# Order of the logits and of the preceding chunk's values inside one TensorE operation of a local attention

## The chip, the cores and the metric

The kernel runs on one core of one Trainium2 chip. The metric is the device time of one execution in microseconds, as the median of several runs. The engines are TensorE (PE in the profile, its weight loads PEld), VectorE (DVE), ScalarE (ACT), GpSimd (POOL) and SyncE (SP), which issues nearly all DMAs.

## The reference, cut to what matters

One decoder layer on x of 2048 tokens by 1024 channels, all in float32. Behind an RMS norm, one projection makes the columns of two head groups that run side by side: a retention (4 heads) and a sliding-window softmax attention (8 query heads, 2 key heads, head size 64, window 128). Each group is gated, the groups are concatenated, projected back and added to x. The change lies in the second group:

```
logits = einsum('bnqhgd,bnkhd->bhgnqk', qb, kband) * 64**-0.5
logits = where(mask, logits + bias, -1e30)          # 0 <= distance < 128
probs  = softmax(concatenate([logits, sink], -1))[..., :-1]
out    = einsum('bhgnqk,bnkhd->bnqhgd', probs, vband)
```

The 2048 tokens are cut into 16 chunks of 128, and a chunk's queries see their own chunk and the one before.

## The kernel before, in words

Four projections (512, 384, 512 and 512 columns wide) take most of the time. Each is made by Strassen's scheme from seven block products for each of 8 pairs of chunks; each of those is 12 matmuls of 128x128 tiles (the float32 operands are split into a high and a low part by ScalarE and VectorE, and three of the four combinations are multiplied). Their results land in PSUM tiles named `acc`; operand tiles are named `x` and `w`. 56 such block products make one projection, and a "turn" in the constants below is one of them.

Between these products TensorE does the small work: transposes, retention (`update`, `retain`) and the local attention (`window`, `attend`, `values`, `outputs`). Small matmuls use parts of the array as separate tiles: the logits (`m<-ks,qT` in the profile) contract 64 rows into 32 columns, the values (`m<-side,vb` and `m<-last,vb`) contract 32 rows into 64 columns, retention uses 64 by 64.

For chunk c, `attend` does this: q is multiplied by its norm's factors on VectorE (`qn`), turned by DMA (`apart`, a store to `planes_dram`, a transposing DMA into `qT`); the keys are turned by TensorE (`m<-ident,kn`) and written by ScalarE into `ks_t`; then one TensorE operation, labelled "logits", is planned for both the values of chunk c - 1 and the logits of chunk c. It takes four PSUM banks `pls`. The logits are 64 matmuls that fill columns 0 to 319 of the banks, banks 0 and 1 in their first half and banks 2 and 3 in their second. The values are 80 matmuls that fill columns 320 to 447: five blocks, one after the other, each over all four banks. Behind it VectorE adds the bias and takes the row's extreme from each bank (`lg<-m,bias,nsnk`, 8 instructions), ScalarE takes the exponential, VectorE turns the blocks (`side`, `last`), and ScalarE copies the four banks' values out (`so`). Chunk 0 has logits alone, and the values of chunk 15 are an operation of their own.

The order of the instructions on every engine is written out ahead, by a planner in the kernel's own code (`Program.emit`). Each operation has a cost for each engine that may do it (how long it occupies the engine, how long until its result is there), a due time in turns, and buffers from pools with shares (`SHARE`). The planner walks through a modelled time and takes the operation that can go first; TensorE's products follow in their fixed order, and small operations are put between them. Where a group of small matmuls follows another such group, it may start `INSIDE` us after its inputs are there; behind a product it is `SETTLED` us. `WIN`, `RET` and `GATE` give the due times of the local attention, of the retention and of the gates, with a base, a step for each chunk or pair, and small amounts by which single ones are moved (`WIN_BY`, `RET_BY`, `GATE_BY`). `EARLIER_Q` moves q's load and its turning ahead of the chunk's due time, `EARLIER_U` does that for retention's state update. `small()` is the planned cost of a small VectorE operation, `VALUES` that of the values.

Every instruction is issued through one helper, so that the profile has line 434 for all of them; groups are told apart by the names of their tiles.

Of the kernel before, what the change touches and what calls it, by code (L numbers as in the profile page):

```python
# [56 lines left out]
CAP = {"k": 93, "h": 8, "bank": 8}  # L57
SMALL, COUNTS = 3, {"ms": 1, "rxt": 1, "rqk0t": 1, "rqk1t": 1}

SHARE = {"x": 14, "raw": 38, "acc": 21, "wr": 20, "wh": 20, "att": 36, "ret": 19, "rin": 14, "gate": 10, "mix": 37, "norm": 7, "res": 6, "turned": 7, "first": 5, "block": 4, "rest": 6}  # L60

HELD = 6
FIRST_X, SPLIT_X = 2.5, 0.4
SHARE["held"] = 2 * HELD

# [34 lines left out]


LATER, CROWD, MOST, SOONER = 15.0, 2.5, 4, 35.0
SETTLED, INSIDE = 0.5, 0.25


def change(a, b):
# [55 lines left out]
class Program:  # L162
# [5 lines left out]
    def op(self, cost, go, r=(), w=(), due=0.0, table=None, label="", also=()):  # L168

        o = Op()  # L170
        o.cost, o.go, o.due, o.after, o.set, o.label = cost, go, due, [], table, label
        o.n, o.left, o.ready, o.end, o.seen, o.by, o.count = len(self.ops), 0, 0.0, 0.0, 0.0, None, 0
        deps = set()
        for b in r:
            if b.writer is not None:
                deps.add(b.writer)
        for b in w:
            if b.writer is not None:
                deps.add(b.writer)
            deps.update(b.readers)  # L180
        for b in r:
            b.readers.append(o)
        for b in w:
            b.writer, b.readers = o, []
        o.bufs = list(dict.fromkeys((*r, *w, *also)))
        for b in o.bufs:
            b.left += 1
        o.new = [b for b in (*w, *also) if b.ap is None and b.tag]
        for d in deps:
            if d is not o:  # L190
                d.after.append(o)
                o.left += 1
        self.ops.append(o)
        return o

    def emit(self):
# [5 lines left out]
        slots = {t: [(0.0, i) for i in range(n)] for t, n in cap.items()}  # L202
        used = dict.fromkeys(SHARE, 0)
        count = len(self.ops)
# [10 lines left out]
        while done < count:  # L215
            best = None
            for e, found in avail.items():
# [4 lines left out]
                for due, n, o in found[:48]:  # L222
# [28 lines left out]
                    for tag, bs in need.items():  # L251
# [7 lines left out]
                        for share in {b.share for b in bs if b.share}:  # L259
                            many = used[share] + sum(b.share == share for b in bs)  # L260
                            if many > SHARE[share] - (spare if share in SPARED else 0):
                                short = True
# [94 lines left out]


TURNED = {"q": range(NCH), "qk": range(NCH), "weights": (), "gated": (2, 4, 6, 7, 10, 12, 14)}
EARLIER_Q, EARLIER_K, EARLIER_U, LATER_W = 0, 1.5, 2.5, -1.0  # L360


def dve(n, two=False, lat=0.08):
# [13 lines left out]


def small(n=1):
    return {"V": (0.14 * n, 0.22 * n, True)}  # L380


def f32r(n, count):
# [4 lines left out]
def f32(n, count):  # L388
    t = count * (n / 600 + 0.01)
    return {"T": (t, t + 0.25, False)}  # L390
# [12 lines left out]
BANDS_DUE, VALUES = 0.0, 1.45  # L403
# [36 lines left out]
def layer(ctx, tc, xt, xfirst, xtok, nw, w_in, w_rn, qkw, sinks, biasg, rope, decays, dmask, gpow, w_out, out):  # L440
    nc = tc.nc
    order = Order(tc)
    V, G, A, Q, T = (Engine(order, e) for e in (nc.vector, nc.gpsimd, nc.scalar, nc.sync, nc.tensor))
# [19 lines left out]
    def kb(name, share, dtype=F32):  # L463
        return Buf("k", None, dtype, name, share)
# [7 lines left out]
    def ps(share="rest", name="m"):  # L472
        return Buf("bank", None, F32, name, share)

    def fixed(shape, name, dtype=F32):
        return Buf(name=name, ap=const.tile(shape, dtype, name=name))
# [11 lines left out]
    def load(b, src, due, kbytes=256, to=lambda t: t, cost=None, also=(), of=lambda t: t):  # L488
        op(
            cost or dma(kbytes), lambda e: e.dma_start(to(b()), of(src())), [src], [b], due, label=f"load {b.name}",  # L490
            also=also,
        )
# [32 lines left out]
    wr = fixed([P, 4], "wr")  # L525
# [359 lines left out]
    def spill(to, n):  # L885
        def sink(p, row, col, b, due):
            store(to[col][2 * p + row], b, due + 4, n // 2, lambda t: t[:, :n])
        return sink
# [347 lines left out]
    def values(c, chunk, vs, banks):  # L1236

        sides, lasts, o, parts = chunk  # L1240

        def go(e):
            by = "p (i q) -> p i q"
            for j in range(5):
                for u, r in enumerate(QUARTERS):
                    for g, to in enumerate((L, H)):
                        v, at = (vs[c], j * P) if j < 4 else (vs[c + 1], 0)
                        if j < 4:
                            w = sides[g]()[r, :].rearrange("p (i k) -> p i k", k=P)[:, :, j * 32 : j * 32 + 32]
                        else:  # L1250
                            w = lasts()[r, o + g * P : o + (g + 1) * P].rearrange(by, q=32)
                        e.matmul(
                            banks[u]()[to, 320 : 320 + P].rearrange(by, q=32), v()[r, at + g * 64 : at + g * 64 + 64], w,
                            start=j == 0, stop=j == 4, skip_group_check=True,
                        )

        return go, [*parts, vs[c], vs[c + 1]], (*sides, lasts)
# [82 lines left out]
    def attend(c, a, b, fac, facs, due, bias_t, ks_t, nsnk, held, vs):  # L1340
# [5 lines left out]
        def go(e):  # L1346
            e.tensor_tensor(
                qn().rearrange(hd, d=HD), a().rearrange(hd, d=HD), fac()[:, 0:8].unsqueeze(2).to_broadcast([P, 8, HD]),
                ALU.mult,
            )  # L1350

        soon = due - (EARLIER_Q if c in TURNED["q"] else 0)
        op(both(512), go, [a, facs], [qn], soon, label="qn")

        def go(e):
            for g in range(KVH):
                e.activation(
                    kn()[:, g * HD : (g + 1) * HD], b()[:, g * HD : (g + 1) * HD], AF.Copy, scale=fac()[:, 8 + g : 9 + g]
                )

        op({"A": (0.47, 0.57, False)}, go, [b, facs], [kn], due, label="kn")

        pk, pq = ps(), ps()
# [6 lines left out]
        if c in TURNED["q"]:  # L1370
            turn_by_dma(qn, qT, planes_dram[2][c], soon + 0.1)
        else:

            def go(e):
                for i in range(4):
                    e.transpose(pq()[:, i * P : (i + 1) * P], qn()[:, i * P : (i + 1) * P], ident())

            op(turns(4), go, [qn, ident], [pq], due + 0.2, "small", label="turn q")
            op({"A": act(512)}, lambda e: e.activation(qT(), pq(), AF.Copy), [pq], [qT], due + 0.35, label="qT")
# [18 lines left out]
        parts = []  # L1398

        pls = [ps() for _ in range(4)]  # L1400
        before, reads, also = values(c - 1, held[-1], vs, pls) if held else (None, [], ())

        def go(e):
            if before:
                before(e)
            for t in range(2):
                for j in range(2):
                    for u, q in enumerate(QUARTERS):
                        for g, r in enumerate((L, H)):
                            o = (2 * t + j) * P + u * 32  # L1410
                            e.matmul(
                                pls[2 * t + g]()[q, j * 160 : j * 160 + 160], qT()[r, o : o + 32],
                                ks_t()[r, slot * 256 + u * 32 : slot * 256 + u * 32 + 160], start=True, stop=True,
                                skip_group_check=True,
                            )

        t = f32(160, 4)["T"][0] + (VALUES - 0.23 if before else 0)
        op(
            {"T": (t, t + 0.25, False)}, go, [qT, ks_t, *reads], [*pls, passed], due + 0.5, "eighths", label="logits", also=also,
        )  # L1420
        for bank, heads in enumerate([(2 * t + j, g) for j in range(2)] for t in range(2) for g in range(2)):
            later, n = due + 0.5 + 0.2 * bank, len(heads)
# [20 lines left out]
            def go(e, lg=lg, heads=heads):  # L1443
# [9 lines left out]
                also=(nm, den),  # L1453
            )
            t, g = bank // 2, bank % 2
            most = Part(sides[g], lambda s, t=t: s[:, t * 256 : t * 256 + 256])
            rest = Part(lasts, lambda s, t=t, g=g: s[:, o + g * P + t * 64 : o + g * P + t * 64 + 64])
# [63 lines left out]
    def gates(p, row, col, b, due):  # L1521

        c = 2 * p + row
        if row == col == 0:
            store(g_dram[p], b, due)
            g = kb("g", "gate")
            due = GATE[0] + p * GATE[1] + GATE_BY[p]
            load(g, g_dram[p], due - 4)
            gate(0, c, due, g)
        else:  # L1530

            need = 3 * n7 + (THREES.at[1 + col, p] if row else THREES.first[6] - 4 + 1.4 * p)
            gate(col, c, max(due + 0.5, GATE[0] + 0.5, need - LEAD), b)

# [45 lines left out]
    products(B1, W1, 384, n7, TWOS, spill(rq_dram, 384))  # L1580
    window(lambda c: WIN[0] + c * WIN[1] + WIN_BY[c])
    retention(lambda c: RET[0] + c // 2 * 2 * RET[1] + c % 2 * 1.0 + RET_BY[c // 2])
    W3 = weights(w_in, 1792, 512, (nw_sb, KT), 2 * n7, TWOS)
# [9 lines left out]


WIN = (47.0, 5.3)
RET = (109.0, 2.85)
GATE = (140.0, 3.8)

WIN_BY = (-1.0, 0.5, -1.5, 0.0, 1.5, 0.5, 1.0, 1.0, -0.5, 1.0, 1.0, 2.0, 0.5, 0.5, 0.0, 2.0)
RET_BY = (-1.5, 0.0, -1.5, 1.0, -1.0, -2.5, -0.5, -1.0)  # L1600
GATE_BY = (-1.5, -0.5, -2.5, -0.5, -0.5, -0.5, 0.0, 0.5)

LEAD = 7.0

# [98 lines left out]
```

## Time and profile before

| | us |
|---|---|
| median of 3 runs | 668.02 (667.99 to 668.63) |
| the profiled execution's own time | 667.38 |
| its span, first to last instruction | 665.6 |
| TensorE busy | 661.2 |
| VectorE busy | 588.2 |
| ScalarE busy | 477.4 |

The page divides the span into 40 slices of 16.6 us. The local attention runs from about 169 to 456 us, the retention from about 314 to 493 us. A row of the timeline gives the start in us from the span's beginning, the time covered in us, the engine, the operation with its tiles and shapes, and a count; brackets hold the engine's idle time just before and what ended it.

### The profile page before, as it was taken

To read this page: it belongs to the slowest core of one execution; us is meant where nothing else is said; L and a number is where in the kernel's file an instruction comes from. 1 tells how busy PE (TensorE), PEld (TensorE's weight loads), DVE (VectorE), ACT (ScalarE), POOL (GpSimd) and SP (SyncE) were. 2 spreads that over 40 slices of the span, in tenths; PEclk is the share of its full clock that TensorE was granted. 3 is DMA by queue.
4 is the path that set the end of the run, shared out by engine and by line. 5 is a ranking of instruction groups with operands and counts; after the bars stand their busy time and mean duration, and the time that the engine had idled before them with its cause. 6 is when DMAs were issued, how large, how long until landed. Compare 5 with 4: busy or idle time off the path is not lost.

```text
span 665.6 us, 16699 instructions
## 1 busy us (share of the span) xinstructions
PE 661.2 (99%) x6072; PEld 561.0 (84%) x6072; DVE 588.2 (88%) x1423; ACT 477.4 (72%) x1177; POOL 15.6 (2%) x39
## 2 busy tenths in 40 slices
PE   9999999999999999999999999999999999999998
PEld 7888888889999999998887888888888888888886
DVE  6999967797788987899999999988899999997862
ACT  7766975577798675698979998999999863353200
POOL 0000000032200000000000000000000000000000
PEclk9999999999999999999999999999999999999999
DMA  9999973789998789999999999898999995126622
GB/s 323 369 327 374 393 258 147 239 305 336 255 312 255 191 257 292 331 302 281 313 286 316 354 268 278 269 261 269 287 308 318 306 282 154 48 95 222 206 95 96
DMA packets 162114, 175.99 MB, mean 264 GB/s; under 512 B 69488, under 2 KB 96240, under 8 KB 162032
## 3 DMA queue, kind: packets, MB, share of 16 engines
q1 hardware_dynamic: 161888, 174.92, 86.7%
q8 instruction: 48, 0.79, 0.5%
q14 instruction: 34, 0.28, 0.1%
q10 hardware_dynamic: 144, 0.00, 0.0%
HBM read 104.03 MB, written 56.43 MB: 241 GB/s over the span
## 4 chain that ended last, share of the span: by engine, by line
PE 99%; DVE 0%; issue 0%
PE acc L434 87%; PE m L434 12%; DVE t L434 0%; DVE none L434 0%
## 5 line engine op out<-in xcount | busy, mean ns | idle before, releaser
L434 PE MATMUL acc<-w,x 128*128 128x512 f32 (+1 forms) x2700 | 588.0, 377 | 0.0
L434 PEld LDWEIGHTS acc<-w,x 128*128 128x128 f32 x2700 | 491.8, 188 | 84.2 <-issue 5.1
L434 DVE TENSOR_TENSOR x<-x 128x512 fp32r<-128x512 f32 (+2 forms) x214 | 140.5, 681 | 9.9 <-ACT x L434 9.5
L434 ACT ACTIVATE x<-x 128x512 fp32r<-128x512 f32 (+1 forms) x181 | 107.2, 616 | 15.2 <-DVE x L434 10.7
L434 DVE TENSOR_TENSOR w<-w 128x512 fp32r<-128x512 f32 (+3 forms) x96 | 61.6, 668 | 0.1
L434 ACT ACTIVATE lg<-lg,nm 128x160 f32<-128x160 f32 x128 | 53.2, 419 | 7.2 <-DVE nm L434 7.1
L434 ACT ACTIVATE w<-w 128x512 fp32r<-128x512 f32 (+1 forms) x72 | 40.9, 602 | 20.8 <-PE acc L434 14.8
L434 DVE TENSOR_TENSOR s<-acc,s 128x512 f32<-128x512 f32 (+1 forms) x64 | 41.8, 654 | 10.0 <-PE acc L434 9.8
L434 DVE SCALAR_TENSOR_TENSOR w<-w,nw_sb 128x512 fp32r<-128x512 f32 (+3 forms) x72 | 49.7, 713 | 0.9 <-ACT w L434 0.9
L434 DVE CUSTOM_DVE_ANT_0 lg<-m,bias,nsnk 128x160 f32<-128x160 f32 x128 | 40.9, 381 | 3.8 <-PE m L434 3.8
L434 DVE TENSOR_TENSOR t<-acc,t 128x512 f32<-128x512 f32 (+2 forms) x33 | 21.0, 636 | 15.9 <-PE acc L434 15.8
L434 ACT ACTIVATE x<-go 128x512 fp32r<-128x512 f32 x40 | 24.2, 630 | 14.8 <-DVE w L434 6.4
L434 ACT ACTIVATE w<-w,nw_sb 128x512 fp32r<-128x512 f32 (+3 forms) x45 | 29.0, 680 | 2.3 <-DMA w<-in_w_in 2.3
L434 DVE STREAM_TRANSPOSE side<-lg 128x256 f32<-128x256 f32 x64 | 28.0, 438 | 2.6 <-ACT lg L434 2.4
L434 DVE TENSOR_TENSOR x<-go,x 128x512 fp32r<-128x512 f32 x40 | 27.5, 694 | 1.1 <-ACT x L434 1.1
L434 ACT ACTIVATE apart<-qn 128x1024 uint16<-128x1024 uint16 x16 | 16.7, 1052 | 14.7 <-DVE qn L434 14.7
L434 DVE TENSOR_TENSOR t<-acc,s 128x512 f32<-128x512 f32 (+1 forms) x32 | 21.3, 665 | 5.1 <-PE acc L434 5.0
L434 ACT ACTIVATE ro<-ro,nmu,rg 128x128 f32<-128x128 f32 x64 | 25.1, 496 | 0.0
L434 DVE TENSOR_TENSOR r<-acc,t 128x512 f32<-128x512 f32 (+1 forms) x32 | 20.9, 653 | 4.4 <-PE acc L434 4.3
L434 ACT ACTIVATION_READ_ACCUMULATOR lg<-lg,nm 128x1 f32 x128 | 24.5, 191 | 0.0
L434 ACT ACTIVATE s<-acc 128x512 f32<-128x512 f32 (+1 forms) x32 | 18.0, 570 | 9.0 <-PE acc L434 8.7
L434 ACT ACTIVATE xk<-xk 128x512 f32<-128x512 f32 x32 | 19.8, 620 | 5.5 <-DMA xk<-in_xtok 5.5
(124 smaller groups left out, 595.1 us busy)
## 6 DMA issues: line engine op xcount, KB each, us to landing
x<-in_xt SPq DMA_DIRECT2D x74, 256.0 KB, 5.2
x<-s_dram SPq DMA_DIRECT2D x64, 256.0 KB, 5.0
planes_dram<-apart SPq DMA_DIRECT2D x55, 256.0 KB, 4.4
w<-in_w_in SPq DMA_DIRECT2D x40, 256.0 KB, 5.4
s_dram<-x SPq DMA_DIRECT2D x32, 256.0 KB, 4.8
xk<-in_xtok SPq DMA_DIRECT2D x32, 256.0 KB, 4.9
res<-in_xtok SPq DMA_DIRECT2D x32, 256.0 KB, 3.8
w<-in_w_out SPq DMA_DIRECT2D x20, 256.0 KB, 4.9
```

The source lines that it names most:

```text
L434: return self.order.put(op(*a, **k))
```

## The change

Inside the common TensorE operation of a chunk, the matmuls of the logits are issued first and those of the preceding chunk's values behind them; both still go to the same four PSUM banks, and the operation still needs all its inputs before it is planned. With it, constants of the planner are changed: two shares of buffers, `INSIDE`, `EARLIER_Q`, `EARLIER_U`, the cost of small VectorE operations, the cost of the common operation, and the due times of retention, of the gates and of one chunk of the window.

```diff
-SHARE = {"x": 14, "raw": 38, "acc": 21, ...
+SHARE = {"x": 15, "raw": 35, "acc": 21, ...
...
-SETTLED, INSIDE = 0.5, 0.25
+SETTLED, INSIDE = 0.5, 0.1
...
-EARLIER_Q, EARLIER_K, EARLIER_U, LATER_W = 0, 1.5, 2.5, -1.0
+EARLIER_Q, EARLIER_K, EARLIER_U, LATER_W = 2.0, 1.5, 1.5, -1.0
...
 def small(n=1):
-    return {"V": (0.14 * n, 0.22 * n, True)}
+    return {"V": (0.17 * n, 0.25 * n, True)}
...
-        before, reads, also = values(c - 1, held[-1], vs, pls) if held else (None, [], ())
+        behind, reads, also = values(c - 1, held[-1], vs, pls) if held else (None, [], ())
 
         def go(e):
-            if before:
-                before(e)
             for t in range(2):
                 for j in range(2):
                     for u, q in enumerate(QUARTERS):
                         for g, r in enumerate((L, H)):
...
+            if behind:
+                behind(e)
+
+        t = f32(160, 4)["T"][0] + (VALUES - 0.31 if behind else 0)
-        t = f32(160, 4)["T"][0] + (VALUES - 0.23 if before else 0)
...
-RET = (109.0, 2.85)
-GATE = (140.0, 3.8)
+RET = (107.0, 2.85)
+GATE = (140.0, 4.0)
...
-WIN_BY = (-1.0, 0.5, -1.5, 0.0, 1.5, 0.5, 1.0, 1.0, -0.5, 1.0, 1.0, 2.0, 0.5, 0.5, 0.0, 2.0)
+WIN_BY = (-1.0, 0.5, -1.5, 0.0, 1.5, 0.5, 1.0, 1.0, -0.5, 1.0, 1.0, 2.0, 0.5, -0.5, 0.0, 2.0)
-GATE_BY = (-1.5, -0.5, -2.5, -0.5, -0.5, -0.5, 0.0, 0.5)
+GATE_BY = (-1.5, 0.5, -1.0, 1.0, 1.0, 1.0, 1.5, 2.0)
```

More of the change, by code (lines that the diff above doesn't have):

```diff
@@ L58 @@
 SMALL, COUNTS = 3, {"ms": 1, "rxt": 1, "rqk0t": 1, "rqk1t": 1}
-SHARE = {"x": 14, "raw": 38, "acc": 21, "wr": 20, "wh": 20, "att": 36, "ret": 19, "rin": 14, "gate": 10, "mix": 37, "norm": 7, "res": 6, "turned": 7, "first": 5, "block": 4, "rest": 6}
+SHARE = {"x": 15, "raw": 35, "acc": 21, "wr": 20, "wh": 20, "att": 36, "ret": 19, "rin": 14, "gate": 10, "mix": 37, "norm": 7, "res": 6, "turned": 7, "first": 5, "block": 4, "rest": 6}
 HELD = 6
```

## The prediction

> **What bounds the kernel now.** I read the page first, then TensorE's waits, then the chain of waits, then the timeline around the changed operation. The page:
>
> ```profile
> span 665.6 us, 16699 instructions
> PE 661.2 (99%) x6072; PEld 561.0 (84%) x6072; DVE 588.2 (88%) x1423; ACT 477.4 (72%) x1177; POOL 15.6 (2%) x39
> PEclk9999999999999999999999999999999999999999
> PE 99%; DVE 0%; issue 0%
> PE acc L434 87%; PE m L434 12%; DVE t L434 0%; DVE none L434 0%
> ```
>
> TensorE is busy for 99% of the span at the full granted clock, and the chain that ends last is TensorE almost alone. A busy TensorE can hide waits, so the list of its waits comes next. It has one entry:
>
> ```profile
> PE m L434 <- DVE none L434: 1.2, 1, 1.2
> ```
>
> That one is the warm-up at the start. After it no matmul waits for data, for a bank or for another engine. So the time is the sum of what TensorE issues, plus the few us at the two ends, and an edit can gain only by taking cycles out of TensorE's own stream; it can lose without limit by making TensorE wait. "Earlier" and "later" on other engines are worth nothing until they reach TensorE.
>
> **The changed operation.** The timeline of TensorE around one instance (the common operation of chunk 2), then the first chunk's logits alone, the last chunk's values alone, and a place where other small matmuls stand in front:
>
> ```profile
> 190.99 1.19 PE L434 MATMUL m<-side,vb 32*64 32x128 f32 x63
> ...
> 192.35 1.34 PE L434 MATMUL m<-ks,qT 64*32 64x160 f32 x64
> 193.62 0.80 PE L434 MATMUL acc<-w,x 128*128 128x384 f32 x3
> ...
> 169.28 1.34 PE L434 MATMUL m<-ks,qT 64*32 64x160 f32 x64
> 170.55 0.80 PE L434 MATMUL acc<-w,x 128*128 128x384 f32 x3
> ...
> 454.69 1.19 PE L434 MATMUL m<-side,vb 32*64 32x128 f32 x63
> ...
> 456.06 0.73 PE L434 MATMUL acc<-w,x 128*128 128x512 f32 x2
> ...
> 313.80 1.10 PE L434 MATMUL m<-v,qk 64*64 64x128 f32 x32
> 314.84 1.19 PE L434 MATMUL m<-side,vb 32*64 32x128 f32 x63
> ...
> 316.20 1.34 PE L434 MATMUL m<-ks,qT 64*32 64x160 f32 x64
> ```
>
> The first column is the start; I count each part from its first start to the next part's, so that it carries the gap behind it. Values: 192.35 - 190.99 = 1.36 us with the logits behind, 456.06 - 454.69 = 1.37 with a product behind, 316.20 - 314.84 = 1.36 with retention's matmuls in front. Logits: 193.62 - 192.35 = 1.27 with the values in front, 170.55 - 169.28 = 1.27 with a product in front. Each part costs the same whoever its neighbours are.
>
> **The swap on TensorE.** It moves 80 value matmuls behind 64 logit matmuls in 15 operations; it adds none and removes none, and moves no DMA by itself. Before: 1.36 + 1.27 = 2.63. After: 1.27 + 1.36 = 2.63, if a part's closing gap depends on that part alone. One seam never occurs in the trace: logits followed by values, from tiles of 64x32 to tiles of 32x64. Its bounds come from retention's matmuls, with a switch of tile size behind them and without:
>
> ```profile
> 398.73 1.10 PE L434 MATMUL m<-v,sT 64*64 64x128 f32 x32
> 399.76 0.74 PE L434 MATMUL acc<-w,x 128*128 128x512 f32 x2
> ...
> 329.55 1.10 PE L434 MATMUL m<-v,sT 64*64 64x128 f32 x32
> 330.48 1.05 PE L434 MATMUL m<-v,qk 64*64 64x128 f32 x32
> 331.46 0.72 PE L434 MATMUL acc<-w,x 128*128 128x512 f32 x2
> ```
>
> With a switch the 32 matmuls take 1.03 us, without one 0.93: a switch costs 0.10. If the new seam had none, each operation would save 0.10, and 15 x 0.10 = 1.5 us; if it cost a second one, it would lose as much. The nearest rows are the two seams into or out of the value matmuls (64x64 to 32x64: 314.84 - 313.80 = 1.04; 32x64 to 64x32: the same 1.36 as to a product). Both pay the switch in full. I take 0.00, and keep -1.5 and +1.5 as ends.
>
> **Stalls inside the operation.** The chain of waits lists the operation in 2.63 us nearly everywhere, and longer in three places:
>
> ```profile
> 250.74 2.63 PE m L434 x142
> 266.18 2.96 PE m L434 x142
> ...
> 287.13 2.76 PE m L434 x141
> ...
> 381.58 2.71 PE m L434 x139
> ```
>
> The excess is 0.33 + 0.13 + 0.08 = 0.54 us. The weight loads show the first as a pause in the middle of the logits, with nothing waited for:
>
> ```profile
> 267.47 0.70 PEld L434 LDWEIGHTS m<-ks,qT 64*32 64x32 f32 x42 [0.17 <-issue]
> 268.40 0.42 PEld L434 LDWEIGHTS m<-ks,qT 64*32 64x32 f32 x22 [0.23 <-issue]
> ```
>
> [...] Ends: all gone (-0.5) or twice as many (+0.5). I take 0.0, the nearest being the same number elsewhere.
>
> **VectorE.** The bias instruction reads the logits' bank. In the old order a bank has its last matmul when its logits are through, and two of the four banks are through halfway:
>
> ```profile
> 208.66 0.38 DVE L434 CUSTOM_DVE_ANT_0 lg<-m,bias,nsnk 128x160 f32<-128x160 f32 x1 [0.93 <-PE m L434]
> ...
> 209.06 0.80 PE L434 MATMUL acc<-w,x 128*128 128x384 f32 x3
> ...
> DVE lg L434 <- PE m L434: 3.8, 4, 1.4
> ```
>
> The first bias of chunk 3 starts at 208.66, 0.40 before the operation's end at 209.06. In the new order the values fill columns 320 to 447 of each bank last of all (the loop over the five value blocks is outside, that over the banks inside), so if the program guards a whole bank, the first bias comes at the operation's end, about 0.45 later than now; if it guards the columns, it comes 1.36 sooner. [...] No row here tells the two apart, and I take the later one. VectorE waits for these logits in 4 chunks only (last row), one of which is chunk 0, without values; the others are 3, 5 and 6. Chunk 2's bias starts before the operation's end as well:
>
> ```profile
> 193.24 0.38 DVE L434 CUSTOM_DVE_ANT_0 lg<-m,bias,nsnk 128x160 f32<-128x160 f32 x1
> ```
>
> (193.24 against 193.62.) Elsewhere the bias comes after the operation and doesn't feel the swap, so 4 x 0.45 = 1.8 us of new waiting on VectorE. Queued behind it are the splits of x and w, which feed the products. What hides it is VectorE's spare time there:
>
> ```profile
> core 0: us, PE busy (x) PEld busy (x) DVE busy (x) ACT busy (x) POOL busy (x), PEclk, DMA share, GB/s
> 175.00:260.00 85.00, 85.00 (x1260) 80.73 (x1259) 73.78 (x234) 65.76 (x212) 0.00 (x0) 1.00 0.91 262
> ...
> 310.00:420.00 110.00, 110.00 (x1612) 88.76 (x1611) 108.03 (x338) 101.76 (x277) 0.00 (x0) 1.00 1.07 298
> ```
>
> In the stage of those chunks it is idle for 85.00 - 73.78 = 11.2 us, so I take 0.0, with +1.8 as the end without cover. From 310 to 420 us it has only 2.0 us to spare, but there the queue ahead of the bias is longer than the operation.
>
> **The planner's constants.** They move no arithmetic, only the order. x gets one more buffer and raw tiles three fewer; q (its loads, the products with its factors, its turning DMAs) goes two turns earlier, retention's base two, its state update one turn later, and the gates up to 2 + 0.2 x 7 = 3.4 turns later; small VectorE operations are planned 0.03 longer; the common operation is planned 0.08 shorter and, next to another small-matmul operation, may follow its inputs by 0.10 instead of 0.25. On SP the 16 q loads (256 KB, 4.7 us to land), 16 stores and 16 turning DMAs come in front of some loads of x:
>
> ```profile
> x<-s_dram SPq DMA_DIRECT2D x64, 256.0 KB, 5.0
> ...
> aq<-aq_dram SPq DMA_DIRECT2D x16, 256.0 KB, 4.7
> ```
>
> TensorE feels any of this in two ways. Neighbouring groups of small matmuls may fuse or come apart: a fusion saves at least the 0.10 of a switch and at most both idle times of the weight loader around a group (0.35 going in, 0.17 coming out, together 0.52):
>
> ```profile
> 398.73 0.86 PEld L434 LDWEIGHTS m<-v,sT 64*64 64x64 f32 x32 [0.35 <-issue]
> 399.76 0.53 PEld L434 LDWEIGHTS acc<-w,x 128*128 128x128 f32 x3 [0.17 <-issue]
> ```
>
> I take 0.2 (an estimate; part of the idle time lies under the product still running). Retention's earlier base brings one more of its steps under the window operations, so I count one fusion more: -0.2. Or a load comes late and TensorE waits: 0.0 here, since it has no wait now; the end is one missed landing of 5.0 us.
>
> **Sum.** 0.0 (seam) + 0.0 (pauses) + 0.0 (VectorE) - 0.2 (order) = -0.2 us against the profiled execution's own 667.4 us (span 665.6 and 1.8 around it): 667.2. The median of the runs is 668.02, 0.6 above that execution, so the forecast on that scale is 667.8 us. A change under 0.2% (1.3 us) can't be told from none by a measurement of this kernel; this is one.
>
> **Rivals.**
> - The seam is free: 1.5 us less, 668.0 - 1.5 - 0.2 = 666.3. For it: the planner now books the operation 0.08 shorter. Against it: all switches in the trace pay. [...] Chance 0.08.
> - The new order is itself the gain: the 0.54 of pauses gone and four more fusions at 0.2, 668.0 - 0.5 - 0.8 = 666.7, at the edge of what is told from none, more if fusions are worth up to 0.52. For it: most retention groups stand apart from the window's. Against it: it needs all of it at once. Chance 0.11.
> - Slower: the bias waits for the whole operation, VectorE stands still for 4 x 0.45 = 1.8 us, and the splits behind reach TensorE late: 668.0 + 1.8 = 669.8. It decides once an operand's split is finished less than 0.45 us before its product. Against it: 11.2 us idle in that stage. Chance 0.11.
> - Slower by SP: one load of x behind the earlier q traffic misses its product by up to a landing: 668.0 + 5.0 = 673.0; the DMA share of 1.07 from 310 to 420 speaks for it, TensorE's empty list of waits against it. Chance 0.07.
> - That the change doesn't do what it says (logits first, readers no earlier) is what I expect, and costs nothing.
>
> **How the numbers follow.** My case, 667.2 to 668.9, has 0.63. The range of 8 in 10 runs from the free seam's 666.3 to the stalled VectorE's 669.8. Faster by over 0.2%: 0.08 + 0.11 = 0.19. Slower: 0.11 + 0.07 = 0.18. Within: 0.63.
>
> **What would show it.** Right: TensorE's list of waits still holds only the warm-up, the logits' first start to the values' is 1.27 and the values' to the next product's 1.36, and the bias of chunk 3 starts at the operation's end or later. The seam fails if the logits take about 1.17 before the values. The VectorE step fails if a bias starts while the value matmuls run. The whole is wrong if TensorE shows a wait for x or w, or if the groups of small matmuls number clearly fewer than now.

## The result, and the profile after

The changed kernel takes 672.03 us (median of 4 runs, 671.45 to 675.22); the kernel before, timed beside it, 668.01 (667.99 to 668.63). The ratio is 1.0071, with a 95% interval of 1.0046 to 1.0097: slower by 4.0 us. I had forecast 667.8 with a range of 666.3 to 669.8, so the forecast and the range were both wrong.

The page of the changed kernel: span, busy times, the chain that ended last by engine, and the group of the bias with the idle time ahead of it.

```profile
span 670.7 us, 16720 instructions
PE 663.1 (99%) x6072; PEld 562.1 (84%) x6072; DVE 587.9 (88%) x1423; ACT 478.4 (71%) x1177; POOL 15.6 (2%) x39
...
PE 84%; ACT 6%; DMA 4%; DVE 3%; issue 2%; SPq 0%; ACTq 0%; DVEq 0%
...
L434 DVE CUSTOM_DVE_ANT_0 lg<-m,bias,nsnk 128x160 f32<-128x160 f32 x128 | 40.8, 380 | 6.1 <-PE m L434 6.1
```

The share of busy time still reads 99%, and no engine has more work: the matmuls are as many (TensorE's busy time is 1.9 us longer for them), VectorE's and ScalarE's busy times are the same within 1 us. What differs is the chain: before, it was TensorE for 99%; now it runs through ScalarE, DMAs and VectorE for 13%, so TensorE waited somewhere. TensorE's list of waits, which held the warm-up alone, names where (us in total, times, longest):

```profile
PE m L434 <- issue: 1.5, 2, 1.0
PE m L434 <- DVE none L434: 1.2, 1, 1.2
PE m L434 <- ACT so L434: 1.1, 1, 1.1
PE acc L434 <- DVE r L434: 0.3, 1, 0.3
```

1.5 + 1.1 + 0.3 = 2.9 us are new. The largest place is one group near 307 us. TensorE's timeline there, then ScalarE's, then VectorE's:

```profile
307.39 1.32 PE L434 MATMUL m<-ks,qT 64*32 64x160 f32 x64
...
310.00 0.43 PE L434 MATMUL m<-v,qk 64*64 64x128 f32 x2
311.41 1.10 PE L434 MATMUL m<-v,qk 64*64 64x128 f32 x30 [0.98 <-issue]
313.62 0.33 PE L434 MATMUL m<-ident,kn 128*128 128x128 f32 x1 [1.12 <-ACT so L434]
313.71 2.54 PE L434 MATMUL acc<-w,x 128*128 128x512 f32 x10
...
310.85 0.41 ACT L434 ACTIVATE lg<-lg,nm 128x160 f32<-128x160 f32 x1
...
313.32 0.74 ACT L434 ACTIVATE so<-m 128x128 f32<-128x128 f32 x4
...
314.46 0.38 DVE L434 COPY state<-m 128x256 f32<-128x256 f32 x1
...
316.48 0.40 DVE L434 TENSOR_TENSOR state<-state,m 128x256 f32<-128x256 f32 x1
317.14 0.41 DVE L434 TENSOR_TENSOR state<-state,m 128x256 f32<-128x256 f32 x1
```

The common operation starts at 307.39. Directly behind it stands retention's first state update (`m<-v,qk`, 32 matmuls), and directly behind that the transpose of the next chunk's keys (`m<-ident,kn`). The update stops after 2 matmuls and goes on at 311.41; the transpose waits until ScalarE begins the four copies `so`, which stand behind six exponentials of 0.41 us. (VectorE takes the update's results out of their two banks later still: from 314.46 on, and as the code reads each bank twice, with the last reads at 316.48 and 317.14.) From the operation's start to the next product it is 313.71 - 307.39 = 6.32 us. Without waits it would be 2.61 + 1.03 + 0.09 = 3.73 (operation, update with its switch, transpose), so 2.6 us are lost.

Before, the same kinds of work met too, in the order update, operation, three matmuls of a product, transpose. The update and the operation (313.80, 314.84 and 316.20) are shown with the prediction; what follows them is

```profile
317.47 0.97 PE L434 MATMUL acc<-w,x 128*128 128x512 f32 x3
318.28 0.27 PE L434 MATMUL m<-ident,kn 128*128 128x128 f32 x1
...
317.17 0.42 DVE L434 TENSOR_TENSOR state<-state,m 128x256 f32<-128x256 f32 x1
```

and nothing waits. There the update stands in front, and the transpose has 318.28 - 314.84 = 3.44 us from the operation's start. By then one of the update's two banks has been read for the last time (the row of VectorE, done at 317.59), so a bank is free without ScalarE's copies; that the transpose takes this bank fits, but no view names the bank.

The weight loader shows smaller waits that the matmuls' list leaves out or counts only in part, these two and one of 0.53 us for ScalarE's `x` at 481:

```profile
357.90 0.97 PEld L434 LDWEIGHTS m<-v,sT 64*64 64x64 f32 x32 [0.40 <-DVE sT L434]
...
394.47 0.86 PEld L434 LDWEIGHTS m<-state,qkT 64*64 64x64 f32 x30 [0.39 <-ACT so L434]
```

The start differs as well. Here are the first products, before and then after:

```profile
4.64 2.53 PE L434 MATMUL acc<-w,x 128*128 128x512 f32 x10
```

```profile
4.79 2.47 PE L434 MATMUL acc<-w,x 128*128 128x512 f32 x5
```

Five matmuls where there were ten, 0.15 us later: about 1.2 us in all. I don't put that down to the change: the same slow start (6 matmuls) is in the profiled execution of a kernel that ran within 0.6 us of the kernel before (the one with the small operations' cost, below), and it is absent (10 matmuls) from the changed kernel with the copies sooner.

The account of the profiled spans, 670.7 - 665.6 = 5.1 us: start +1.2; the group at 307 +2.6; a pause of 0.9 in the operation at 267 against three pauses of 0.54 in all before +0.4; the place at 394 +0.6 and the one at 480 +0.5; waits for masked scores `sT` at 358, 378 and 488 +0.3; the swap itself -0.4 (see the seam, in the section on the prediction). That makes 5.2. The groups of small matmuls, counted in TensorE's timeline, are 33 in both executions, so no fusion enters. The medians differ by 4.0; the account without the start gives as much.

### The profile page after: what moved, and what is told of

Its sections match the earlier page's. It is cut to its first block, busy times and chain, and to the rows that moved or that the text cites. A ratio compares the mean times of both kernels' runs of the same rounds, so it can differ in the third digit from the quotient of the medians.

```text
span 670.7 us, 16720 instructions
## 1 busy us (share of the span) xinstructions
PE 663.1 (99%) x6072; PEld 562.1 (84%) x6072; DVE 587.9 (88%) x1423; ACT 478.4 (71%) x1177; POOL 15.6 (2%) x39
## 4 chain that ended last, share of the span: by engine, by line
PE 84%; ACT 6%; DMA 4%; DVE 3%; issue 2%; SPq 0%; ACTq 0%; DVEq 0%
PE acc L434 76%; PE m L434 8%; DMA planes_dram<-apart 2%; ACT ro L434 1%; ACT lg L434 1%; ACT qk L434 1%; ACT apart L434 1%; DVE w L434 1%; DMA so_dram<-so 1%; DMA w<-in_w_in 1%; ACT x L434 1%; DMA a<-rq_dram 1%; DMA v<-rq_dram 0%; DVE lg L434 0%; ACT w L434 0%
```

## The experiments

Each kernel was timed beside the kernel before; ratios are to that one, with 95% intervals. The first question was whether the order inside the operation costs anything, or the plan around it.

**The swap alone.** The kernel before, with nothing changed but the order of the two parts; all constants, and so the order on every engine, are those of before.

```diff
         def go(e):
-            if before:
-                before(e)
             for t in range(2):
...
+            if before:
+                before(e)
```

> The kernel before with the swap of the matmuls alone: logits first, values behind, every constant of the planner and so every engine's order as before. Theory A (the new plan of the order is what costs): TensorE's operation takes 2.70 us instead of 2.73 by the trace of after, 15 x 0.025 = 0.4 us less, the bias of chunk 3 starts about 0.5 us later, and the whole stays within 1 us of 668.0. Theory B (the swap costs, since the bias and then the copies of the values are held until the operation's end and the banks come free later): 670 to 672 us, with waits of TensorE for ScalarE's copies.

Measured: 667.92 us, ratio 0.9997 (0.9983 to 1.0011). TensorE's one wait besides the warm-up's, and the first bias of chunk 3:

```profile
PE m L434 <- issue: 0.4, 1, 0.4
...
209.27 0.38 DVE L434 CUSTOM_DVE_ANT_0 lg<-m,bias,nsnk 128x160 f32<-128x160 f32 x1 [1.17 <-PE m L434]
```

The bias starts at 209.27 instead of 208.66, 0.6 later, and VectorE waits longer, but TensorE doesn't feel it. In the profiled execution most operations take 2.61 us instead of 2.63, 0.4 us less in all, and two take 3.25 and 3.09 because of pauses. The swap costs nothing and gains nothing that can be told.

**The plan alone.** The changed kernel with the values first again: all constants as changed, the order of the engines as changed.

```diff
         def go(e):
+            if behind:
+                behind(e)
             for t in range(2):
...
-            if behind:
-                behind(e)
```

> The changed kernel with its own plan, but the values first again inside the operation. Theory A (the plan costs): 671 to 672 us, with the pause near 269 us, the pause near 310 us and the waits for the copies near 313 and 394 us still there. Theory B (the swap costs): 668 to 669 us, the waits for the copies gone, because the bias starts 0.4 us or more before the operation's end again.

Measured: 672.82 us, ratio 1.0072 (1.0051 to 1.0093), as for the whole change. TensorE's timeline:

```profile
307.63 1.19 PE L434 MATMUL m<-side,vb 32*64 32x128 f32 x63
...
310.27 1.22 PE L434 MATMUL m<-v,qk 64*64 64x128 f32 x32
313.87 0.39 PE L434 MATMUL m<-ident,kn 128*128 128x128 f32 x1 [2.38 <-ACT so L434]
313.96 4.34 PE L434 MATMUL acc<-w,x 128*128 128x512 f32 x11
```

Again 313.96 - 307.63 = 6.33 us for the group, now without a pause in the update: the transpose waits 2.38 in one piece. So the loss belongs to the changed constants, and the update's pause in the changed kernel only takes time out of a wait that is there anyway. Behind the wait, 11 matmuls take 4.34 us, where 10 took 2.54 in the changed kernel; more on that in the last section.

**Where the pause comes from.** Four matmuls of 256 columns at the start (the warm-up, `WARM` in the code), whose result nothing reads, are replaced by sixteen of 64 columns; the stream of instructions behind them is 48 longer and otherwise the same.

```diff
-        for _ in range(WARM):
-            e.matmul(pw()[:, 0:256], none()[:, 0:P], none()[:, 0:256], start=True, stop=True)
+        for i in range(4 * WARM):
+            e.matmul(pw()[:, 0:64], none()[:, 0:P], none()[:, 0:64], start=True, stop=True)
```

> The changed kernel with the 4 warm-up matmuls of 256 columns replaced by 16 of 64 columns; the order of everything behind is the same, but TensorE's instruction stream is 48 instructions longer ahead of the first product. If the pauses with nothing waited for (0.9 us in the values near 269 us and 1.4 us in retention's matmuls near 310 us) are fetches of instructions, they move or vanish: the next block is asked for 24 matmuls earlier in the stream, 4 us in the products, so both should be gone, 2.3 us, if no other place gets one: 669 to 670 us. If they are waits for data or banks, they stand at the same matmuls with the same lengths, and the time stays 671 to 672 us.

Measured: 676.83 us, ratio 1.0135 (1.0118 to 1.0152). The warm-up itself got dearer: the first product starts at 8.03 us instead of 4.79, and more of the first ones are slow (11 matmuls from 9 to 13 us, where the changed kernel has 19), so the whole time, which I had expected at 669 to 670 us, says nothing about the rest. The places do:

```profile
273.58 1.19 PE L434 MATMUL m<-side,vb 32*64 32x128 f32 x63
...
274.95 0.80 PE L434 MATMUL acc<-w,x 128*128 128x384 f32 x3
...
311.66 1.32 PE L434 MATMUL m<-ks,qT 64*32 64x160 f32 x64
...
314.27 1.10 PE L434 MATMUL m<-v,qk 64*64 64x128 f32 x32
317.96 0.33 PE L434 MATMUL m<-ident,kn 128*128 128x128 f32 x1 [2.59 <-ACT so L434]
```

Both pauses are gone, the one in the values (273.58 to 274.95 is the undisturbed 1.37) and the one in the update, and yet the transpose comes 317.96 - 311.66 = 6.30 us behind the operation's start, no sooner than in the changed kernel (313.62 - 307.39 = 6.23). So the wait is not made by the pauses. That the fetch of instructions makes them is a guess of mine; no view shows a fetch. For it speaks, beside the two that are gone here, where the pause in the operation at 267 us stands: behind its 120th matmul in the changed kernel, and again on the same stream in the kernel with the light exponentials. Against a fixed pause speaks its length there, below.

**The copies sooner.** ScalarE's copies `so` are planned 0.7 turns earlier.

```diff
-            outputs(c - 1, pls, [[n] for n in nms[-4:]], due + 1.2)
+            outputs(c - 1, pls, [[n] for n in nms[-4:]], due + 0.5)
```

> The changed kernel with the copies of the values out of the banks due 0.7 turns sooner (0.5 instead of 1.2 behind the chunk's due time), so that ScalarE does them between the exponentials rather than behind six of them; the planner makes a new order of it. If the late release of the banks costs, the waits of TensorE for the copies (1.2 us near 313, 0.6 near 394) go, 1 to 2 us less than 672.0. If not, the time stays within what a new order does anyway, 670 to 673 us, with or without those waits.

Measured: 672.53 us, ratio 1.0050 (1.0026 to 1.0073). The copies now go two by two between the exponentials, the first two at 310.56, and the transpose doesn't wait. But a pause has come into the update:

```profile
308.99 0.65 PE L434 MATMUL m<-v,qk 64*64 64x128 f32 x10
311.45 1.55 PE L434 MATMUL m<-v,qk 64*64 64x128 f32 x22 [1.82 <-ACT so L434]
```

The view names `so` as what ended it, but an update that has issued 10 of its 32 matmuls already has its banks; so I take it for a pause like the one behind 2 matmuls in the changed kernel's update, uncovered this time. From this run alone that can't be settled. The next product comes at 313.06, 313.06 - 306.38 = 6.68 us behind the operation's start, so of the 1 to 2 us that I had expected nothing came, and by itself this run doesn't show that the late copies cost anything.

**The exponentials light.** The changed kernel's order, but each exponential handles 32 of its 160 columns, and its argument is scaled to nothing: four fifths of the softmax's exponentials and their row extremes are left out.

```diff
-                        lg()[:, at : at + 160], lg()[:, at : at + 160], AF.Exp, scale=-1.0,
-                        bias=nm()[:, c % SETTLE, h : h + 1], accum_out=den()[:, c % SETTLE, h : h + 1],
+                        lg()[:, at : at + 32], lg()[:, at : at + 32], AF.Exp, scale=-1e-30,
+                        accum_out=den()[:, c % SETTLE, h : h + 1],
```

> The changed kernel with the same order on every engine; left out is four fifths of each exponential (32 of 160 columns, of a scaled-down argument and without the row's extreme), so its output isn't the reference's. ScalarE then needs about 0.31 us for one instead of 0.41, and the copies behind six of them come about 0.6 us sooner. If TensorE waits for the banks that these copies give back, its wait near 313 us falls from 1.2 to about 0.6 us and the one near 394 from 0.3 to nothing, and ScalarE's splits come sooner too: 670 to 671 us. If ScalarE has nothing to do with it, the waits stay and the time is 671.5 to 673.

Measured: 670.49 us, ratio 1.0031 (1.0015 to 1.0047). TensorE, then ScalarE:

```profile
308.07 1.32 PE L434 MATMUL m<-ks,qT 64*32 64x160 f32 x64
...
310.68 1.10 PE L434 MATMUL m<-v,qk 64*64 64x128 f32 x32
...
313.19 0.33 PE L434 MATMUL m<-ident,kn 128*128 128x128 f32 x1 [1.41 <-ACT so L434]
...
312.88 0.76 ACT L434 ACTIVATE so<-m 128x128 f32<-128x128 f32 x4
```

The copies start 312.88 - 308.07 = 4.81 us behind the operation's start instead of 5.93, 1.1 sooner where I had expected 0.6 (an exponential starts every 0.21 us here, instead of 0.41 in the changed kernel and the 0.31 that I had put), and the transpose comes as much sooner; the places at 358, 394 and 480 wait no longer (a wait of 0.4 for `sT` at 325 is new). So ScalarE's work ahead of the copies sets the waits: 1.1 of the 2.6 us here, and about half of the whole loss. The pauses behave otherwise. TensorE's stream is that of the changed kernel, and yet the update runs in one piece here, while the pause in the operation at 267 is 1.29 us long instead of 0.52. Whether and how long TensorE pauses thus differs between executions of one and the same stream, and the longer stream's undisturbed update, one execution too, proves less than it seems to.

**The update away from the operation.** In the changed kernel the first update must wait for the keys that the transpose turns (by a buffer that holds nothing), so that the transpose goes first.

```diff
+    eleventh = Buf(name="eleventh", ap=())
...
-            f32(P, 4), go, [held_up, *(b for ...
+            f32(P, 4), go, [held_up, *([eleventh] if c == 0 else []), *(b for ...
...
-            turns(1), ..., [kn, ident, passed], [pk], due + 0.2, "small",
+            turns(1), ..., [kn, ident, passed], [pk, eleventh] if c == 11 else [pk], due + 0.2, "small",
```

> The changed kernel, with one dependency more: retention's first state update waits for the turned keys of chunk 11, so it can't be planned right behind the common operation near 307 us; the order behind that place changes with it. Theory A (the update right behind the operation costs, because the keys' transpose behind both then needs a bank that ScalarE's copies haven't given back): the operation near 307 takes 2.7 us up to the next product instead of 6.4 for the group, the wait of TensorE for the copies there goes, and the time falls by about 2.5 us, to 669.5. Theory B (the loss is spread over the whole plan): within 1 us of 672.

Measured: 674.25 us, ratio 1.0078 (1.0051 to 1.0105). TensorE's timeline:

```profile
309.48 1.32 PE L434 MATMUL m<-ks,qT 64*32 64x160 f32 x64
...
312.09 0.96 PE L434 MATMUL acc<-w,x 128*128 128x512 f32 x3
312.89 0.27 PE L434 MATMUL m<-ident,kn 128*128 128x128 f32 x1
```

At the place itself it is as expected: the transpose comes 3.41 us behind the operation's start and waits for nothing, although the copies come only at 317.66. So the transpose doesn't need the copies as such; it lacks a bank when the update's two banks (`kvs` in the code) are taken beside the operation's four. That makes six, and six banks are all that `SHARE` allows the small work (`rest`). But the planner answered with another order later on, and waits of 1.5 us for `so` near 392 and 1.0 for VectorE's `x` near 351 took the place. My expectation for the time was a miss.

**The transpose a little later.** The changed kernel with the transpose made to wait for the copies in the plan, so that products come before it.

```diff
-            turns(1), ..., [kn, ident, passed], [pk], due + 0.2, "small",
+            turns(1), ..., [kn, ident, passed, *(copied[9] if c == 11 else ())], [pk], due + 0.2, "small",
```

> The changed kernel, but the keys' transpose of chunk 11 (the one right behind the group near 307 us) must wait for ScalarE's copies of chunk 9's values, so that the written order puts one block product (12 matmuls, 2.7 us) between retention's first state update and that transpose; what comes after 350 us is ordered a little differently too. Theory (the group's 6.41 us are one bank wait, with a pause in the instruction stream lying beneath it): the operation and the update take 3.7 us from start to the product, or up to 5.1 if the pause of up to 1.4 us, now uncovered, stays; the transpose waits less than 0.3; the whole is 1.3 to 2.6 us below the changed kernel, 669.4 to 670.7 us, if no later wait grows. Rival (any order of the changed constants makes a wait of this size somewhere): the group is shorter, but the sum of TensorE's waits after 350 us grows by as much, and the time stays at 671.5 to 674 us. Rival (the operation followed by the update is itself dear): the group still takes over 6 us without the transpose.

Measured: 674.09 us, ratio 1.0069 (1.0045 to 1.0092). TensorE, then ScalarE:

```profile
306.34 1.32 PE L434 MATMUL m<-ks,qT 64*32 64x160 f32 x64
...
308.95 1.14 PE L434 MATMUL m<-v,qk 64*64 64x128 f32 x32
310.01 0.96 PE L434 MATMUL acc<-w,x 128*128 128x512 f32 x3
312.55 0.33 PE L434 MATMUL m<-ident,kn 128*128 128x128 f32 x1 [1.58 <-ACT so L434]
...
312.25 0.73 ACT L434 ACTIVATE so<-m 128x128 f32<-128x128 f32 x4
```

The operation and the update take 310.01 - 306.34 = 3.67 us, as theory had it: the two side by side are not dear. But I had read the written order wrongly: only 3 matmuls (0.7 us) came between, not 12, and they didn't cover the wait. The transpose still comes when the copies do, 312.55 - 306.34 = 6.21 us behind the operation's start (6.23 in the changed kernel, 6.24 in the plan alone, 6.30 with the longer stream). For the whole time the rival was right: a second wait for `so` of 1.8 us came at 393 and one for `ro` of 1.1 at 362.

**Which constants.** Four kernels are the kernel before with the swap and one edit each: the operation's planned cost, the small operations' planned cost, the gates (with `GATE_BY` as in the change), and the shares (with chunk 13's due time in `WIN_BY` as in the change):

```diff
-        t = f32(160, 4)["T"][0] + (VALUES - 0.23 if before else 0)
+        t = f32(160, 4)["T"][0] + (VALUES - 0.31 if before else 0)
...
-    return {"V": (0.14 * n, 0.22 * n, True)}
+    return {"V": (0.17 * n, 0.25 * n, True)}
...
-GATE = (140.0, 3.8)
+GATE = (140.0, 4.0)
...
-SHARE = {"x": 14, "raw": 38, ...
+SHARE = {"x": 15, "raw": 35, ...
```

A fifth is the whole change except `INSIDE`, `EARLIER_Q`, `EARLIER_U`, `RET` and the operation's cost, which are those of before.

> The kernel before with the swap and one constant: the common operation is planned 0.08 us shorter, as in the changed kernel; all other constants as before. In the planner's order this is enough to put retention's first state update right behind the common operation. Theory A (that place is the cost): TensorE waits there again for ScalarE's copies, the group up to the next product takes 6 us or more, and the time is 670 to 671.5 us. Theory B (another constant is the cost): 668 us, as with the swap alone.

> The kernel before with the swap and one constant: small VectorE operations planned 0.03 us longer. The planner's order changes on VectorE, ScalarE and SP and little on TensorE; the first update stays in front of an operation. If only the update behind the operation costs, 668 to 669 us, like the swap alone. If any new order of the crowded stage costs, 669.5 to 672 us, with some waits of TensorE for ScalarE or VectorE between 310 and 580 us.

> The kernel before with the swap and the gates' due times of the changed kernel, up to 3 turns later; all else as before. Theory: later gates move ScalarE's and VectorE's work behind 400 us and cost little, 668 to 669 us. Rival (any new order costs, or the gates come too late for the last projection): 669.5 to 672 us, with waits of TensorE for x made from the gated tiles (near 480 or from 515 us on).

> The kernel before with the swap, chunk 13 of the window due one turn sooner and the two shares of buffers as in the changed kernel; the smallest change of the order among these. If any new order costs, 669 to 670.5 us; if it takes a particular one, 668 us as with the swap alone.

> The changed kernel with four of its constants as before (the planned cost of the common operation, the 0.25 behind another small group, the earlier q and update, and retention's base); the swap, the shares, the small operations' cost, the window's and the gates' due times stay changed. In the planner's order the first update is no longer behind the common operation. Theory A: no group of 6 us, 668 to 669.5 us. Theory B (the shares, the gates and the rest cost): 671 us or more, with waits of TensorE in the stage of the gates, from 410 us on.

Measured: operation's cost 1.0101 (1.0059 to 1.0143); small operations 1.0011 (0.9998 to 1.0024); gates 1.0021 (1.0008 to 1.0033); shares and one chunk 0.9995 (0.9982 to 1.0008); the rest 1.0054 (1.0035 to 1.0073). 0.08 us in one planned cost put the update behind the operation all by itself and cost as much as the whole change:

```profile
310.58 0.97 PE L434 MATMUL m<-v,qk 64*64 64x128 f32 x25 [2.30 <-issue]
311.57 0.82 PE L434 MATMUL acc<-w,x 128*128 128x512 f32 x2
```

(The operation starts at 305.23, so the group takes 6.34 us again. The pause of 2.30 inside the update covers the wait: the copies begin at 311.24, and the transpose follows at 311.49, 6.26 us behind the start.) The time, 674.54 us, is above the 670 to 671.5 that I had expected: a wait of 1.35 us for `rg` at 372 and a slower clock (a mean of 0.995 to 0.999 in the four executions) come on top. The gates, at 669.95, also cost more than the 668 to 669 that I had expected, by waits of 1.1 us for VectorE's `x`. The rest, without this group, was a clear miss: I had expected at most 669.5, and it took 672.20, with waits of 0.9 us for ScalarE's `x`, 0.9 for VectorE's, 0.6 for `sT` and 0.5 for `go`. A new order as such needn't cost anything, as the shares show.

**All runs side by side.** TensorE's waits of the profiled execution by its list, without the warm-up's 1.2, against the median's distance from the kernel before beside it:

| kernel | waits, us | median minus before, us |
|---|---|---|
| shares and one chunk | 0.6 | -0.7 |
| swap alone | 0.4 | -0.3 |
| small operations' cost | 0.2 | +0.5 |
| gates | 1.5 | +1.5 |
| light exponentials | 3.1 | +2.1 |
| rest of the constants | 3.3 | +3.2 |
| the change | 2.9 | +4.0 |
| copies sooner | 3.5 | +4.3 |
| plan alone | 3.5 | +4.6 |
| update away | 4.2 | +5.3 |
| transpose later | 4.5 | +5.4 |
| operation's cost | 3.7 | +5.6 |

The kernel with the longer stream is left out, for its warm-up. Few waits, no loss; from 2.9 us of waits on, the loss is 2 to 5.6 us, whatever engine is named in them. It is not exact: the list leaves out most of what the weight loader waits for, each row is one execution, and in the profiled executions of three of the kernels (copies sooner, plan alone, operation's cost) a slower clock comes on top, told in the last section. No kernel beat the one before by more than its interval.

## Why the prediction was wrong

- **TensorE's stream sets the time, and it had no wait: right**, and with it the sentence that an edit "can lose without limit by making TensorE wait". What it could lose was then priced for two mechanisms only, VectorE's and SP's.
- **The seam pays in full: right.** In the changed kernel, chunk 2's operation is

```profile
192.23 1.32 PE L434 MATMUL m<-ks,qT 64*32 64x160 f32 x64
193.48 1.19 PE L434 MATMUL m<-side,vb 32*64 32x128 f32 x63
...
194.84 0.80 PE L434 MATMUL acc<-w,x 128*128 128x384 f32 x3
...
210.25 0.39 DVE L434 CUSTOM_DVE_ANT_0 lg<-m,bias,nsnk 128x160 f32<-128x160 f32 x1 [1.31 <-PE m L434]
...
210.25 0.80 PE L434 MATMUL acc<-w,x 128*128 128x384 f32 x3
```

  193.48 - 192.23 = 1.25 and 194.84 - 193.48 = 1.36: 2.61 instead of 2.63. A free seam would have shown about 1.17 for the logits. The 0.02 to 0.03 in 15 operations are the -0.4 us of the account.
- **The bias comes at the operation's end: right**, and here the runs tell what no row before did. The last two rows above are chunk 3's first bias and the first product behind the operation: both start at 210.25, the bias behind 1.31 us of waiting for TensorE, though it reads columns 0 to 319 and the values write columns 320 to 447. In this program the bias is held by the values' matmuls on the other columns of its bank as well. VectorE's waiting for logits went from 3.8 to 6.1 us in the changed kernel, 2.3 more where I had put 1.8.
- **That waiting reaches TensorE (the first slower rival): not seen.** With the swap alone VectorE waits 4.8 us, and the time is the same. The cover that I named, VectorE's 11.2 idle us, was enough.
- **The pauses inside the operation, 0.0: too low** by 0.4 (0.9 at 267 us against 0.54 in three places). That another order has the same number of them, no run shows: with the swap alone the pauses made two operations 3.25 and 3.09 us long instead of 2.61, and on the changed kernel's stream the one at 267 us was 0.52 us in one execution and 1.29 in another, the one with the light exponentials.
- **The planner's constants: the step that failed.** I wrote that they "move no arithmetic, only the order", and priced the order as "one fusion more: -0.2", with one late load as the only way to lose. No fusion came: the groups of small matmuls are 33 before and after, and the first update stood beside a common operation before as well. What the order did was to put the update behind the operation and the keys' transpose behind both, and this costs 2.6 us instead of saving 0.2. The reason is not the meeting as such: update and operation side by side took 3.67 us in the run with the later transpose. It is that operation and update together hold six banks, all that the small work has. ScalarE begins to empty the first of them behind VectorE's biases and six exponentials, 5.9 us after the operation's start (the update's own two are free only after 316.48 and 317.14, over 9 us after it), while the matmuls in between last only 3.7. The light exponentials moved the copies and the transpose together by 1.1 us, which shows the chain; the update taken away made the transpose free, which shows the banks.
- **A misreading, without effect on the sum:** the gates go up to 1.5 + 0.2 x 7 = 2.9 turns later, not 3.4.
- **The second slower rival, a load of x late by SP: a wrong place.** Sixteen q loads and turning DMAs were to be late; what came late was what ScalarE and VectorE make in the crowded stage: copies, masked scores `sT`, splits `x`. VectorE's idle time from 310 to 420 us, of which I noted only 2.0 us in the kernel before, was the warning row; I used it for the bias alone.
- **What the old trace could have told.** Not the place of the wait, but its likelihood: from 310 to 420 us VectorE and ScalarE were busy for 108.03 and 101.76 of 110 us, and TensorE waited for neither. An order with so little to spare is easily made worse, and constants that reorder that very stage deserved a chance of slower well over 0.18.

What stays open: the costs of the constants don't add up. The operation's cost alone costs 1.0101, everything but five constants 1.0054, the whole change 1.0071. I know a place and a price for each order that was run, but no rule for which constants make a bad order. Only the place at 307, 2.6 of the some 4 us, was taken apart by runs; no run with the changed constants came back to the time before, as new waits took the place of the old ones. What makes the pauses no run shows: instruction fetch is my guess from the place of one of them in the stream and from the two that were gone with the longer one, and one was missing without any shift.

## What to carry to other kernels

Where the bounding engine has no wait at all, a change that reorders its neighbours isn't worth the cycles it saves but the waits it makes: price each group of small matmuls by how long its PSUM banks are held (here 5.9 us until ScalarE began to empty the first), not by its matmuls (3.7 us). Separate an edit of the code from the retuning that comes with it and time each alone; here the edit made no difference that could be told and the retuning cost 4 us. A busy share of 99% doesn't show such waits: TensorE's list of waits and the share of other engines in the chain do.

## What the runs showed of the hardware that was not expected

**A wait can cost more than its length.** In the plan alone, TensorE's granted clock falls behind the wait of 2.38 us. The rows give the time, then the busy us of each engine with counts, and then the clock, the DMA share and GB/s. The plan alone comes first, then the changed kernel:

```profile
314.00:315.00 1.00, 1.00 (x4) 0.81 (x5) 1.00 (x5) 1.00 (x6) 0.00 (x0) 0.50 0.73 209
...
317.00:318.00 1.00, 1.00 (x5) 0.79 (x4) 1.00 (x3) 0.49 (x2) 0.00 (x0) 0.79 1.96 299
```

```profile
314.00:315.00 1.00, 1.00 (x6) 0.80 (x5) 1.00 (x5) 1.00 (x6) 0.00 (x0) 1.00 1.04 295
```

From 314.0 to about 317.4 us the clock is 0.50, and so about 1.7 us more are lost (an estimate, half of 3.4 us). The same happened at this place in the profiled executions of the kernel with the copies sooner (idle 1.82, then a clock of 0.50 from 312 to 314 us) and the one with the operation's cost (idle 2.30, then 0.51 and 0.50 from 312 to 315 us); it didn't in those of the kernel with the longer stream (idle 2.59, a clock of 1.00 from 315 to 330 us) and of the changed kernel (idle 0.98 and 1.12). But it is a matter of the execution more than of the kernel. One such stretch in 672 us makes a mean clock of about 0.997, and that was the mean in 2 of 4 executions of the changed kernel, 3 of 4 with the longer stream, 3 of 4 of the plan alone and 4 of 8 with the copies sooner; the swap alone, with 10 executions, has none below 0.999. The length of the idle time alone doesn't decide it: 1.82 to 2.38 us were followed by the slower clock, and 2.59 us were not. What does, no run here shows.

**The clock column doesn't show the start.** The five slow matmuls of the changed kernel behind 4.79 us run at half pace, 2.47 us for 5 where 10 took 2.53 before, with a granted clock that reads 1.00 in both. There the count of matmuls tells, not the column; what slows them no view shows.
